# First norm and input tiles in another order, squares summed in pairs, context's row later, eight banks in the first rows, input weights by GpSimd's queue

## The chip, the cores and the metric

The kernel runs on one core of a Trainium2 chip. The metric is the device time of one execution in microseconds (us), taken as the median of several runs. Profiles and traces come from one profiled execution each.

## The reference

One block of a hybrid diffusion backbone on 512 latent tokens and 256 context tokens of width 2048, all in fp32. Only its beginning matters here:

```python
mod_l = (silu(c) @ w_ada + b_ada)          # 6 x 2048: shift, scale, gate, twice
mod_c = (silu(c_ctx) @ w_ada + b_ada)
h_l = rms_norm(x, g_mix_norm) * (1 + sc_a) + sh_a
h_c = rms_norm(ctx, g_mix_norm) * (1 + csc_a) + csh_a
qa, kva, kr, cb, cc, ch = split(h_l @ w_in)   # 2048 -> 3968 columns (31 tiles of 128, key rope twice)
...                                        # attention beside a gated convolution, output projection,
...                                        # second norm and modulation, gated MLP, final norm
```

## The kernel before

Activations lie transposed: a tile is 128 features by 512 tokens, x is sixteen of them (xs, NK = 16). Products are exact to fp32 by splitting both sides into a rounded part (hi, a cast on ScalarE) and a remainder (lo, a subtraction on VectorE) and adding three matmuls, hi-hi, hi-lo and lo-hi (mm3, lines 187 to 189). Weights are loaded into two buffers (load, tile raw), split four blocks at a time into four pairs of buffers and a spare one (split, lines 166 and 167).

At the start c is spread over the partitions by matmuls with ones and put through silu (silu_rows, lines 413 and 414), the sixteen tiles are loaded, squared on ScalarE and added up one by one on VectorE (add_squares, lines 351 to 355), context's row is treated as c was, and the norm's factor is made by rms: sums across partitions by matmuls (line 316), root and reciprocal, spread by transposes (line 299), copy to rl.

Each input tile j is then prepared by prep(j): ada(16 + j) and ada(j) load a 1 MB row of w_ada each, in two halves into four buffers (tag ada), and VectorE multiplies each half by sv = silu(c) with an accumulated sum (dot_v, line 241: four products per tile); modulate(j) scales the tile by rl (line 435), applies scale and shift on ScalarE (line 438) and splits it (hilo, lines 337 and 338).

The input projection runs in three parts of 2, 4 and 10 input tiles (KCH), each over all 31 column tiles in the order ORDER:

```python
KCH = [2, 4, 10]
K0 = [0, 2, 6]
```

In each part the first G = 6 column tiles go row by row, input tile by input tile as these become ready, on six half banks (first_banks, names pf); the other 25 go column tile by column tile (names pp). Results of the first part are copied out by ScalarE (acc), later parts are added to acc by VectorE (evac). Tiles 2 to 15 are prepared between the column tiles by the table todo, and the third part also multiplies all rows of w_ada by svc = silu(c_ctx) (ctx_mods).

Within each engine the order is set by a scheduler that goes by dependencies, except where keep() fixes it; the fetches of this stage are kept in program order on SyncE's queue (fetch_to, line 145), the weights (names rf, rw) among the modulation rows (names ada). sv is also stored to memory once, for the MLP's gate (line 1009).

## Time and profile before

| | |
|---|---|
| median of 3 runs (lowest, highest) | 2137.75 us (2131.43, 2138.17) |
| profiled execution, its own time | 2139.37 us |
| its span | 2137.6 us |
| mean granted TensorE clock, share of full | 0.993 |
| busy: TensorE, VectorE, ScalarE, GpSimd | 2091.0, 1826.5, 1047.5, 117.2 us |
| moved by DMA | 513.75 MB, 240 GB/s over the span |

The busy time of an engine is the sum over the whole execution; shares differ much between stages. The first 100 us, in which the norm is made and the input projection starts, are the stage that the change touches. In the trace's names PE is TensorE (PEld its weight load), DVE is VectorE, ACT is ScalarE, POOL is GpSimd, SP is SyncE, and a name with q is that engine's queue.

### The profile page before, as it was taken

How to read it: one execution, taken by the hardware profiler on the slowest of the kernel's cores; microseconds unless marked ns; L12 is line 12 of the kernel's file. 1: busy time of each engine (PE TensorE's matmuls, PEld its weight loads, DVE VectorE, ACT ScalarE, POOL GpSimd, SP SyncE). 2: the span in 40 equal slices, each digit the busy share in tenths (PEclk: the TensorE clock that was granted, in tenths of full speed). 3: DMA queues.
4: the chain of work that ended last, by engine and by line, in shares of the span. 5: the costliest groups of instructions: out<-in, count | busy, mean ns of one | idle time of the engine just before them, and what ended most of it. 6: DMA issues, size and time to landing. Idle time of an engine off the chain costs nothing.

```text
span 2137.6 us, 35318 instructions
## 1 busy us (share of the span) xinstructions
PE 2091.0 (98%) x13268; PEld 1881.8 (88%) x13268; DVE 1826.5 (85%) x3024; ACT 1047.5 (49%) x1715; POOL 117.2 (5%) x144
## 2 busy tenths in 40 slices
PE   7999999999999999999999999999999999999997
PEld 4688788888988888999999999999999889999997
DVE  7998987778896989898999999999999658888887
ACT  5533333555552337565555555555655433333445
POOL 0000000000000100011000000000000000000000
PEclk9999999999999999999999999999999999999999
DMA  8989886334459986577788888788888989878684
GB/s 331 343 279 329 276 275 195 126 128 152 166 188 353 348 283 220 142 217 207 230 238 232 233 233 244 224 234 234 235 229 229 362 306 307 250 231 239 197 236 134
DMA packets 170177, 513.75 MB, mean 240 GB/s; under 512 B 18963, under 2 KB 23315, under 8 KB 164371
## 3 DMA queue, kind: packets, MB, share of 16 engines
q1 hardware_dynamic: 133364, 418.14, 57.7%
q0 software_dynamic: 17408, 59.25, 14.1%
q10 hardware_dynamic: 19232, 34.09, 4.2%
q8 instruction: 104, 1.70, 0.3%
q14 instruction: 69, 0.56, 0.1%
HBM read 464.22 MB, written 46.14 MB: 239 GB/s over the span
## 4 chain that ended last, share of the span: by engine, by line
PE 90%; DVE 4%; DMA 3%; ACT 2%; issue 1%; SPq 0%; DVEq 0%; ACTq 0%; POOLq 0%
PE pp L187 4%; PE pp L189 4%; PE pp L188 4%; PE d L187 1%; PE o L187 1%; PE d L188 1%; PE o L188 1%; PE d L189 1%; PE o L189 1%; PE uf L187 1%; PE uf L189 1%; PE uf L188 1%; PE of L187 1%; PE of L188 1%; PE of L189 1%; PE pf L188 1%
## 5 line engine op out<-in xcount | busy, mean ns | idle before, releaser
L1151 POOL DMA_DIRECT2D u_s<-in_w_up x80 | 68.6, 857 | 684.0 <-DMA u_s<-in_w_up 378.1
L263 DVE SCALAR_TENSOR_TENSOR ada<-ada,sv 128x1024 f32<-128x1024 f32 x68 | 82.1, 1220 | 11.4 <-DMA ada<-in_w_ada 11.2
L166 ACT CAST w_0h<-rw 128x512 fp32r<-128x512 f32 (+1 forms) x63 | 38.3, 618 | 108.3 <-PE pp L188 67.6
L241 DVE SCALAR_TENSOR_TENSOR ada<-ada,sv 128x1024 f32<-128x1024 f32 x64 | 77.6, 1220 | 2.2 <-DMA ada<-in_w_ada 2.1
L530 DVE SCALAR_TENSOR_TENSOR ada<-ada,svc 128x1024 f32<-128x1024 f32 x64 | 76.0, 1219 | 2.5 <-DMA ada<-in_w_ada 2.4
L167 DVE TENSOR_TENSOR w_0l<-rw,w_0h 128x512 fp32r<-128x512 f32 (+1 forms) x63 | 42.7, 683 | 22.8 <-ACT w_0h L166 22.6
L263 DVE SCALAR_TENSOR_TENSOR ra<-ra,sv 128x1024 f32<-128x1024 f32 x44 | 52.5, 1219 | 1.1 <-DMA ra<-in_w_ada 1.1
L1265 DVE TENSOR_TENSOR u<-u,u_s 128x1024 f32<-128x1024 f32 x40 | 48.8, 1220 | 0.7 <-DMA u_s<-in_w_up 0.5
L1266 DVE TENSOR_TENSOR u<-u,u 128x1024 f32<-128x1024 f32 x40 | 48.7, 1218 | 0.0
L793 POOL TENSOR_TENSOR gr<-gr,half 128x8 f32<-128x8 f32 x4 | 10.1, 2524 | 630.1 <-DVE gr L792 538.2
L764 ACT CAST pth<-t 128x384 fp32r<-128x384 f32 x64 | 28.6, 485 | 26.4 <-PE t L761 26.4
L1075 DVE TENSOR_TENSOR tp<-a,tp 128x256 fp32r<-128x256 f32 x90 | 37.7, 419 | 3.3 <-ACT tp L1074 3.3
L1074 ACT CAST tp<-a 128x256 fp32r<-128x256 f32 x90 | 35.7, 403 | 5.5 <-DMA yl6h<-y_d 4.2
L1038 ACT ACTIVATE g<-g 128x512 f32<-128x512 f32 x43 | 27.3, 634 | 18.3 <-DVE g L1032 18.0
L541 DVE TENSOR_TENSOR acc<-acc,pp 128x512 f32<-128x512 f32 x50 | 34.1, 683 | 2.1 <-PE pp L189 2.1
L765 DVE TENSOR_TENSOR ptl<-t,pth 128x384 fp32r<-128x384 f32 x64 | 33.2, 550 | 2.6 <-ACT pth L764 2.6
L745 DVE TENSOR_REDUCE mn<-s 128x1 f32<-128x768 f32 x32 | 30.4, 953 | 4.9 <-PE s L734 4.6
L1030 ACT ACTIVATE g<-cg,sm 128x512 f32<-128x512 f32 x40 | 32.6, 815 | 0.0
L1030 ACT ACTIVATE a<-ca,sm 128x512 f32<-128x512 f32 x40 | 32.1, 802 | 0.0
L748 ACT ACTIVATE p<-s,mn 128x768 f32<-128x768 f32 x32 | 29.3, 916 | 1.6 <-DVE mn L745 1.3
L1031 DVE SCALAR_TENSOR_TENSOR g<-cg,sm,g 128x511 f32<-128x511 f32 x40 | 29.8, 746 | 0.0
L1032 DVE SCALAR_TENSOR_TENSOR g<-cg,sm,g 128x511 f32<-128x511 f32 x40 | 29.8, 746 | 0.0
(10238 smaller groups left out, 8925.0 us busy)
## 6 DMA issues: line engine op xcount, KB each, us to landing
ada<-in_w_ada SPq DMA_DIRECT2D x196, 512.0 KB, 5.7
u<-in_w_up SPq DMA_DIRECT2D x120, 512.0 KB, 8.9
w<-t_d SPq DMA_DIRECT2D x161, 256.0 KB, 5.3
u_s<-in_w_up SPq DMA_DIRECT2D x80, 512.0 KB, 4.0
u_s<-in_w_up POOLq DMA_DIRECT2D x80, 512.0 KB, 9.6
t_d<-tp ACTq DMA_DIRECT2D x126, 256.0 KB, 5.9
v<-in_w_dnw SPq DMA_DIRECT2D x72, 384.0 KB, 5.1
ra<-in_w_ada SPq DMA_DIRECT2D x22, 1024.0 KB, 4.8
```

What stands on the lines that cost most here:

```text
L166: A.copy(out=hi[:, :n], in_=raw[:, a:a + n])
L167: V.tensor_tensor(out=lo[:, :n], in0=raw[:, a:a + n], in1=hi[:, :n].bitcast(F32), op=ALU.subtract)
L187: PE.matmul(ps, w[0], x[0], start=first, stop=False, skip_group_check=on_top)
L188: PE.matmul(ps, w[0], x[1], start=False, stop=False, skip_group_check=on_top)
L189: PE.matmul(ps, w[1], x[0], start=False, stop=last, skip_group_check=on_top)
L241: V.scalar_tensor_tensor(out=r, in0=r, scalar=1.0, in1=vec[:, i * 1024:(i + 1) * 1024], op0=ALU.mult, op1=ALU.mult, accum_out=col[:, i:i + 1])
L263: keep(V.scalar_tensor_tensor(out=r, in0=r, scalar=1.0, in1=svs[i], op0=ALU.mult, op1=ALU.mult, accum_out=lc[:, t % 4:t % 4 + 1] if i else ...
L530: keep(V.scalar_tensor_tensor(out=raw[q], in0=raw[q], scalar=1.0, in1=svc[:, q * 1024:(q + 1) * 1024], op0=ALU.mult, op1=ALU.mult, accum_o ...
L1030: A.activation(u, src, AF.Identity, bias=s("fb", m), scale=s("fw", 86 + m))
L1151: G_.dma_start(r[-1], src[more], accum_op=ALU.add)
L1265: V.tensor_tensor(out=a11, in0=a11, in1=s1, op=ALU.add)
L1266: V.tensor_tensor(out=a12, in0=a12, in1=a11, op=ALU.add)
```

## The change

- The constants and c are fetched by ScalarE's queue; SyncE's begins with the input tiles. The two halves of modulation row 16 go between tiles 9 and 12, those of row 0 behind tile 15, then the small constants and the first weights in two halves.
- Squares: tiles 5, 9 and 13 are squared by VectorE, the others by ScalarE; two squares are added, and the pair's sums across partitions are taken at once by four matmuls that accumulate. The table for the root is loaded early.
- The first tile has a function of its own, first_tile, in a fixed order: it is scaled by the spread factor straight from the bank, and the activation is done twice, once into the rounded part. A small copy on GpSimd waits for row 0's result, ahead of that queue's loads.
- In the first part eight column tiles go row by row (GCH = [8, 6, 6]), so 23 are left; the array w_in is laid out accordingly. The casts of this part's other weights are held behind the second tile's split.
- Context's row is fetched at the second part's start, spread over the partitions by the fetch itself, and put through silu in one activation after that part's first rows.
- All further weights of the input projection are fetched by GpSimd's queue.
- The store of sv keeps its place in program order, at the end of the output projection.

```diff
+GCH = [8, 6, 6]
...
-    def first_banks(nm):
-        turn[:] = 5, None
+    def first_banks(nm, n):
+        turn[:] = (5 if n == 6 else 0), None
         r = [sml(f"{nm}{g}") for g in range(4)]
-        b = big(f"{nm}4")
-        return r + [b[:, :512], b[:, 512:]]
+        for g in range(4, n, 2):
+            b = big(f"{nm}{g}")
+            r += [b[:, :512], b[:, 512:]]
+        return r
...
-        fetch_to(raw[:, :n], src)
+        if E is not None:
+            keep(E.dma_start(raw[:, :n], src))
+        elif halves:
...
+        def first_tile():
+
+            for t in (16, 0):
+                keep(total(cols[t], t, mod[:, t:t + 1]))
+            keep(G_.tensor_copy(out=tiny(1, "late"), in_=mod[:, 0:1]))
+            sc = tiny(1, "sc0")
+            scale_of(sc, s("g_mix", 0), mod[:, 16:17])
+            x = xs[0]
+            keep(V.tensor_tensor(out=x, in0=x, in1=rs[:, 512:], op=ALU.mult))
+            hi, lo = (t2([P, T], F32R, f"h0{z}") for z in "hl")
+            w = [split_hi(raw0, 0, 512, "wf_0")]
+            keep(A.activation(hi, x, AF.Identity, bias=mod[:, 0:1], scale=sc))
+            keep(A.activation(x, x, AF.Identity, bias=mod[:, 0:1], scale=sc))
+            for a in (4, 8, 12):
+                w.append(split_hi(raw0, a * P, 512, f"wf_{a}"))
+            keep(A.copy(out=rl, in_=rs[:, 512:]))
+            split_lo(*w[0])
+            keep(V.tensor_tensor(out=lo, in0=x, in1=hi.bitcast(F32), op=ALU.subtract))
+            for z in w[1:]:
+                split_lo(*z)
+            hl[0] = hi, lo
+            return [part(z[:2], q) for z in w for q in range(4)]
...
-        for j in range(NK):
...
-            ssq = add_squares(ssq, xs[j], T, f"xs{j}")
-        silu_rows(c_ctx, svc, "cc")
...
+        for j in range(0, NK, 2):
+            q = square(j)
+            if j == 2:
+                for g in range(4):
+                    keep(A.activation(sv[:, g * 512:(g + 1) * 512], cps[g], AF.Silu))
+            r = square(j + 1)
+            if j == 12:
+                keep(A.activation(tiny(1, "root"), eps, AF.Sqrt))
+            keep(V.tensor_tensor(out=q, in0=q, in1=r, op=ALU.add))
+            for g in range(4):
+                PE.matmul(rs[:, g:g + 1], q[:, g * P:(g + 1) * P], ones[:, 0:1], start=j == 0 and g == 0, stop=j == NK - 2 and g == 3)
+            if j in (10, 12):
+                dot_half(16, j // 2 - 5, cols[16])
+        rr = tiny(4, "rr")
+        keep(A.activation(rr, rs[:, :4], AF.Sqrt, bias=eps, scale=1.0 / D))
+        keep(V.reciprocal(rr, rr))
+        spread(rs[:, 512:], rr)
+        for i in range(2):
+            dot_half(0, i, cols[0])
...
+            if ci == 1:
+                fetch_to(svc, c_ctx[0].partition_broadcast(P))
...
-                    raw = load(w_in[:, off:off + 2 * G * P], 2 * G * P, f"rf{ci}{q}")
...
+                        raw = load(w_in[:, off:off + 2 * Gc * P], 2 * Gc * P, f"rf{ci}{q}", G_)
...
+                keep(A.activation(svc, svc, AF.Silu))
...
-                    raw = load(w_in[:, off:off + k * P], k * P, f"rw{ci}_{m}")
...
+                    raw = load(w_in[:, off:off + k * P], k * P, f"rw{ci}_{m}", G_)
...
+                    with ExitStack() as behind_made:
+                        if ci == 0:
+                            for ins in second:
+                                behind_made.enter_context(tc.issue_after(ins))
...
-    SP.dma_start(sv_d, sv)
+    keep(SP.dma_start(sv_d, sv))
```

On VectorE, from the last squares to the first tile, the program before has this (xs0t the running sum, ada the halves of rows 16 and 0, rr the norm's factor):

```order
L355 TENSOR_TENSOR xs0t<-xs0t,xs_184 128x512
L455 TENSOR_SCALAR sm<-sm 128x4
L355 TENSOR_TENSOR xs0t<-xs0t,xs_189 128x512
L241 SCALAR_TENSOR_TENSOR ada_227,dvl_231<-ada_227,sv 128x1024
L241 SCALAR_TENSOR_TENSOR ada_229,dvl_231<-ada_229,sv 128x1024
L235 SCALAR_TENSOR_TENSOR mod<-dvl_231,sm 128x1
L241 SCALAR_TENSOR_TENSOR ada_235,dvl_239<-ada_235,sv 128x1024
L282 SCALAR_TENSOR_TENSOR sc_244<-mod,sm 128x1
L241 SCALAR_TENSOR_TENSOR ada_237,dvl_239<-ada_237,sv 128x1024
L235 SCALAR_TENSOR_TENSOR mod<-dvl_239,sm 128x1
L291 RECIPROCAL rr<-rr 128x4
L167 TENSOR_TENSOR wf_0l<-rf_251,wf_0h 128x512
```

The same place now, up to the scaling of the first tile by the factor in the bank rs:

```order
L526 SCALAR_TENSOR_TENSOR ada_134,dvl_159<-ada_134,sv 128x1024
L519 TENSOR_TENSOR xs_222<-xr_144 128x512
L537 TENSOR_TENSOR xs_220<-xs_220,xs_222 128x512
L526 SCALAR_TENSOR_TENSOR ada_140,dvl_159<-ada_140,sv 128x1024
L537 TENSOR_TENSOR xs_232<-xs_232,xs_234 128x512
L544 RECIPROCAL rr<-rr 128x4
L526 SCALAR_TENSOR_TENSOR ada_150,dvl_160<-ada_150,sv 128x1024
L526 SCALAR_TENSOR_TENSOR ada_152,dvl_160<-ada_152,sv 128x1024
L244 SCALAR_TENSOR_TENSOR mod<-dvl_159,sm 128x1
L244 SCALAR_TENSOR_TENSOR mod<-dvl_160,sm 128x1
L293 SCALAR_TENSOR_TENSOR sc_262<-mod,sm 128x1
L449 TENSOR_TENSOR xr_114<-xr_114,rs 128x512
```

Two of the four products now stand among the squares, and the reciprocal ahead of the other two.

On ScalarE at the second tile (xr the tile under activation, h1h its rounded part, w_..h weight casts, acc a copy out of a bank), before:

```order
L438 ACTIVATE xr_117<-xr_117,mod,sc_300 128x512
L166 CAST w_13_0h<-rw_13_337 128x512
L166 CAST w_15_0h<-rw_13_337 128x512
L166 CAST w_17_0h<-rw_13_337 128x512
L337 CAST h1h<-xr_117 128x512
L539 COPY acc_325<-pf_222 128x512
```

And now:

```order
L479 ACTIVATE xr_116<-xr_116,mod,sc_328 128x512
L481 CAST h1h<-xr_116 128x512
L175 CAST w_15_0h<-rw_15_375 128x512
L175 CAST w_17_0h<-rw_15_375 128x512
L175 CAST w_23_0h<-rw_23_511 128x512
L631 COPY acc_359<-pf_252 128x512
```

The tile's cast has moved ahead of three weight casts.

On SyncE's queue around the start of the second part, before (rf weights, ada modulation halves, kc constants):

```order
L145 DMA ada_854<-in_w_ada 128x1024
L145 DMA ada_921<-in_w_ada 128x1024
L145 DMA rf_717<-in_w_in 128x1536
L145 DMA ada_923<-in_w_ada 128x1024
L145 DMA ada_929<-in_w_ada 128x1024
L145 DMA ada_931<-in_w_ada 128x1024
L145 DMA rf_767<-in_w_in 128x1536
L145 DMA kc<-in_consts 128x1152
```

The weights of the first and second part now stand on GpSimd's queue, behind a copy that waits for row 0's result:

```order
L445 COPY late<-mod 128x1
L159 DMA rw_15_375<-in_w_in 128x2048
L159 DMA rw_23_511<-in_w_in 128x2048
L159 DMA rw_6_623<-in_w_in 128x1792
L159 DMA rf_734<-in_w_in 128x1536
L159 DMA rf_784<-in_w_in 128x1536
L159 DMA rw_13_842<-in_w_in 128x2048
```

SyncE's queue keeps the modulation halves, and the two rf loads that stood among them have moved to the other queue.

## Rows read from the trace of the kernel before

**Rows 1.** The page: the chain that ended last, shares of the span by engine.
```profile
PE 90%; DVE 4%; DMA 3%; ACT 2%; issue 1%; SPq 0%; DVEq 0%; ACTq 0%; POOLq 0%
```

**Rows 2.** Windows: width, busy us (instructions) by engine, granted clock, DMA share, GB/s.
```profile
0.00:10.00 10.00, 5.57 (x6) 1.94 (x7) 2.01 (x5) 6.59 (x10) 0.20 (x4) 1.00 0.75 242
10.00:20.00 10.00, 6.28 (x8) 2.11 (x7) 8.83 (x15) 8.17 (x16) 0.00 (x0) 1.00 1.04 402
20.00:30.00 10.00, 6.11 (x17) 3.50 (x16) 9.02 (x19) 6.25 (x11) 0.00 (x0) 1.00 1.02 416
30.00:40.00 10.00, 9.23 (x27) 6.17 (x26) 8.54 (x18) 2.89 (x5) 0.00 (x0) 1.00 0.82 326
40.00:50.00 10.00, 10.00 (x43) 8.15 (x44) 8.58 (x18) 4.95 (x9) 0.00 (x0) 1.00 0.81 257
50.00:60.00 10.00, 6.86 (x22) 4.67 (x21) 8.56 (x15) 5.34 (x10) 0.00 (x0) 0.76 1.01 403
60.00:80.00 20.00, 17.69 (x70) 13.42 (x69) 17.32 (x38) 11.20 (x21) 0.00 (x0) 0.95 0.81 272
80.00:100.00 20.00, 19.04 (x82) 15.12 (x82) 18.56 (x38) 12.64 (x22) 0.00 (x0) 1.00 1.01 399
100.00:120.00 20.00, 20.00 (x88) 16.21 (x87) 20.00 (x38) 6.56 (x12) 0.00 (x0) 1.00 0.83 281
160.00:200.00 40.00, 40.00 (x174) 32.43 (x173) 33.15 (x65) 17.18 (x30) 0.00 (x0) 1.00 0.90 311
```

**Rows 3.** Timeline of the first 40 us: start, duration, engine, line, operation, idle before.
```profile
1.58 9.56 SPq L145 DMA_DIRECT2D xr<-in_xt  x16
...
8.68 10.25 DVE L355 TENSOR_TENSOR xs0t<-xs0t,xs 128x512 f32<-128x512 f32 x13 [1.73 <-ACT xs L354]
...
19.64 1.22 DVE L241 SCALAR_TENSOR_TENSOR ada<-ada,sv 128x1024 f32<-128x1024 f32 x1
...
22.76 1.86 PE L316 MATMUL rs<-io,xs0t 128*128 128x1 f32 x8
...
23.48 1.28 ACT L289 ACT_TABLE_LOAD   x1
...
25.31 1.11 PE L299 MATMUL rs<-io,rr 128*128 128x128 f32 x4 [0.68 <-DVE rr L291]
...
28.11 0.81 ACT L438 ACTIVATE xr<-xr,mod,sc 128x512 f32<-128x512 f32 x1 [1.04 <-DVE xr L435]
...
29.63 2.07 PE L187 MATMUL pf<-h0h,wf_0h 128*128 128x512 f32 x4 [3.21 <-ACT h0h L337]
...
35.67 1.65 ACT L166 CAST w_0h<-rw 128x512 fp32r<-128x512 f32 x3
...
37.89 0.73 PE L187 MATMUL pf<-h1h,wf_4h 128*128 128x512 f32 x2 [0.33 <-ACT h1h L337]
```

**Rows 4.** The chain in order of time, at 44 us: start, duration, piece.
```profile
43.96 8.89 DMA rw<-in_w_in
```

**Rows 5.** DMA issues of the whole execution: count, KB each, median us to landing.
```profile
u_s<-in_w_up SPq DMA_DIRECT2D x80, 512.0 KB, 4.0
u_s<-in_w_up POOLq DMA_DIRECT2D x80, 512.0 KB, 9.6
t_d<-tp ACTq DMA_DIRECT2D x126, 256.0 KB, 5.9
...
rw<-in_w_in SPq DMA_DIRECT2D x25, 640.0 KB, 6.2
...
x_d<-x POOLq DMA_DIRECT2D x14, 256.0 KB, 6.3
```

**Rows 6.** Tiles h2 and h6, their pp matmuls: durations, first and last start.
```profile
L188 PE MATMUL pp<-h2l,w_0h x25: 390/393/404, 104.5 to 172.4; 128*128 128x512 f32 x25
...
L188 PE MATMUL pp<-h6l,w_0h x25: 390/392/404, 216.1 to 398.0; 128*128 128x512 f32 x25
```

**Rows 7.** The page: a costly group, busy us and mean ns, idle before.
```profile
L167 DVE TENSOR_TENSOR w_0l<-rw,w_0h 128x512 fp32r<-128x512 f32 (+1 forms) x63 | 42.7, 683 | 22.8 <-ACT w_0h L166 22.6
```

More of the change, by code (lines that the diff above doesn't have):

```diff
@@ L147, in fetch_to, with load @@
             keep(ins)
-    def load(src, n, name):
+    def load(src, n, name, E=None, halves=False):
         nth["raw"] += 1
@@ new lines, in block_kernel, with square @@
+        for j in range(10):
+            x_load_in(j)
+        ada_half(16, 0)
+        for j in (10, 11):
+            x_load_in(j)
+        ada_half(16, 1)
+        for j in range(12, NK):
+            x_load_in(j)
+        ada_half(0, 0)
+        ada_half(0, 1)
+        fetch_to(sm, small)
+        raw0 = load(w_in[:, :2 * GCH[0] * P], 2 * GCH[0] * P, "rf00", halves=True)
+        rs = big("rs")
+        def square(j):
+            q = tmp([P, T], F32, f"xs{j}")
+            if j in (5, 9, 13):
+                keep(V.tensor_tensor(out=q, in0=xs[j], in1=xs[j], op=ALU.mult))
+            else:
+                keep(A.activation(q, xs[j], AF.Square))
+            return q
@@ new lines, in dot_half @@
+        def dot_half(t, i, col):
+            r = ada_0[t, i]
+            keep(V.scalar_tensor_tensor(out=r, in0=r, scalar=1.0, in1=svs[i], op0=ALU.mult, op1=ALU.mult, accum_out=col[:, i:i + 1]))
+        cols = {t: tiny(2, f"dvl{t}") for t in (16, 0)}
+        for j in range(0, NK, 2):
[11 more added lines that the diff above has]
+                dot_half(16, j // 2 - 5, cols[16])
```

83 lines of the change are left out of this document (53 added, 30 removed).

## The prediction

> **What bounds the kernel now.** I read the chain that ended last first: TensorE has 90% of it [rows 1], so a microsecond comes off only where TensorE waits or runs slowly. The windows show where that is. From 100 us on, TensorE does 88 matmuls in 20.00 us, 0.227 us each, with no gap; between 30 and 100 us it does 27, 43, 22, 70 and 82, together 244, where that rate gives 308 [rows 2]. That is 64 matmuls or 14.5 us lost, and all of the change's arithmetic lies in or before this stretch. VectorE is the second engine to watch: it is busy 20.00 of 20 us right behind it (100 to 120), has 8.4 us idle between 30 and 100, and 6.9 us between 160 and 200 [rows 2].
>
> The timeline says what the first matmul waits for. The sixteen input tiles are fetched first; VectorE adds their squares one by one, thirteen adds in 10.25 us, and only when that ends, near 19.7 us, does it turn to the modulation products (1.22 each). Sums across partitions start at 22.76, are held by a table load (23.48, 1.28), and are spread at 25.31 in 1.11. The first matmul starts at 29.63 and the first of the second tile at 37.89, behind three weight casts that stand at 35.67 ahead of that tile's own cast [rows 3]. Later the chain goes through one weight load: issued by SyncE at 43.96, it took 8.89 us [rows 4]. Around it the window 50 to 60 has 22 matmuls and a mean granted clock of 0.76, a mixture of the 2.4 and 1.2 GHz levels, and 60 to 80 has 0.95 [rows 2].
>
> **The change part by part.**
>
> *Start of the first tile.* By 10 us the transfers moved 242 GB/s over 10 us, 2.42 MB, and 402 to 416 GB/s after that [rows 2]. SyncE's first input load stood at 1.58 behind the constants and c [rows 3]; these go to ScalarE's queue, and I take 0.8 us for it. The constants (0.13 MB), sixteen tiles (4.19 MB) and the two halves of modulation row 16 now sent among them (1.05 MB) make 5.37 MB: 9.2 + (5.37 - 2.42)/0.402 = 16.5 us until the last tile is there. Then one square, as long as a cast (0.6), one pair's add (0.69) end at 17.8. Four sum matmuls instead of eight and no table load take the stretch from 22.76 to the reciprocal (about 2.5 before the spread at 25.31) down to 1.4: half of 1.86 goes, and the rest of the table load behind it. The reciprocal ends near 19.2. Row 0's halves land at 16.5 + 1.05/0.402 = 19.1. VectorE's two products on them (2.44), which the order puts behind the reciprocal, end at 21.7; the spread (1.11) runs beside them. Three tiny operations and the scaling of the tile, 1.3 together, reach 23.0; the activation now writes the rounded tile itself (0.81). First matmul: about 24.0 instead of 29.63, and the first weights (behind row 0, the small constants and with their own half 7.2 MB in all) are due at 9.2 + (7.2 - 2.42)/0.402 = 21.1, so not late. The pairs take 11 operations instead of 15 from VectorE; that lies under the loads and I count it as nothing: without that cover it is 4 x 0.69 = 2.8.
>
> *The second tile.* What is late next is VectorE. Behind the scaling it has five remainders (0.68 each, one waits for the second activation, which ends at 24.7), to 27.6; then four products (4.9), three tiny ones (0.5) and the scaling (0.7), to 33.7. The activation and the tile's cast, which the order now puts ahead of the weight casts (1.65 for three), take 0.81 and 0.6. That gives 35.3 against 37.89: 2.6 us. By the order 24 instead of 18 matmuls stand ahead of it, since eight banks are used; six more done is 6 x 0.227 = 1.4. **Term one: 2.6 + 1.4 = 4.0**, between 1.4 (the second tile no earlier) and 5.6 + 1.4 = 7.0 (the whole of the start kept).
>
> *Weight loads by GpSimd's queue.* 42 loads leave SyncE's queue, where each waits behind the modulation loads in front of it and they behind it. The second weight load can go when the first buffer's last remainder is done, 27.6 us; with the issue and even the 8.89 us of [rows 4] it lands near 37, and TensorE needs it some 40 matmuls after 35.3. So the stop around 52 us goes: 3.1 us idle in the window 50 to 60, and the low clock, 0.24 x 10 + 0.05 x 20 = 3.4 us [rows 2]. **Term two: 6.5**, between 0 (the load is as late there) and 9.8 (the other idle time of 60 to 100, 2.3 + 1.0 us, goes too). The order keeps ScalarE's copies between casts, to which that remaining idle time belongs, so I keep it at 6.5.
>
> How long does a plain load by GpSimd's queue take? The trace has none. A plain store by it took 6.3 us, one of the same size by ScalarE's queue 5.9, a ratio of 1.07; the accumulating load of u_s took 9.6 against 4.0 by SyncE, a ratio of 2.4 [rows 5]. Applied to the 6.2 us of a 640 KB weight load, that is 6.6 or 14.9 us. These loads do not accumulate, so I take 6.6. In the long third part a block of weights is used up in (398.0 - 216.1)/24 = 7.58 us [rows 6]; with two buffers the landing and about 2.3 us of casts and remainder (1.65 + 0.68 [rows 3, 7]) must fit into 2 x 7.58, so a landing of up to 12.8 us costs nothing.
>
> VectorE runs without a gap while many of these loads are issued [rows 2], and the trace shows no plain load by this queue beside it. The Trainium skill, SBUF — State Buffer, Summary: rules for kernel authors, advises against this very move: descriptors of GpSimd's queue can't be written while VectorE holds the port the two share, so loads that are to hide beside VectorE belong on another queue. By it the time would be that of the slower rival below; by the stores' row it is that of this sum. The same page, Who interferes with whom, has copies and tensor_scalar take that port for descriptors and not tensor_tensor, and VectorE here runs products, subtractions and adds, which is why I give it a small chance only.
>
> *What it costs.* (a) Between 32 and 35.3 us TensorE has nothing to do: 24 matmuls, the first dozen at half rate as the 27 of the window 30 to 40 suggest, end near 32. Whether the clock falls again I cannot see; after the stop at 52 it did, for 3.4 us. **Term three: -1.7**, between 0 and -3.4. (b) Context's row comes as 1.05 MB spread over the partitions instead of 8 KB, 2.6 us of transfers near 65 us, and its silu, with a table load (1.28), sits on ScalarE as one block of about 3 us ahead of the cast of tile 7. VectorE then idles some 2 to 3 us. Tile 7 is first used in the third part, near 170 us, so this comes out of VectorE's 6.9 us there and costs nothing; without that cover 3 us. (c) The store of sv, 1.05 MB, moves from 16 us to ahead of the up projection's first weights: 0 to 2.6 us, and since those loads stand in the queue anyway I take **term four: -0.3**. The four matmuls of context's row leave TensorE before 23 us, where it waits anyway: nothing.
>
> Sum: 4.0 + 6.5 - 1.7 - 0.3 = **8.5 us less**. The profiled execution took 2139.37 us (span 2137.6), so 2130.9; the median of the three runs is 1.6 below it, so **2129.2**, written 2129.
>
> **The rivals.**
> - *VectorE takes it back.* Its work up to the end of the second part is the same, and at the second tile it is only about 1.5 us ahead of before (27.6 with the first tile's remainder done, against 28 without). Only if its 8.4 us of gaps close can it follow TensorE. These depend on the same transfers: up to 100 us 33.9 MB were moved [rows 2], which at 402 GB/s takes 84 us, so there is room, but not much. If the gaps stay, TensorE stands at VectorE's adds in the second part and keeps 1.5 to 4 us: **2135**. For it speaks the full 100-to-120 row, against it the 6.9 us idle behind.
> - *TensorE runs through.* If clock and remaining idle time also come right, 4.0 + 9.8 = 13.8: **2124**. It needs the transfers near 402 GB/s throughout.
> - *Slower: weights late from GpSimd's queue.* With 14.9 us for a landing a block takes (14.9 + 2.3)/2 = 8.6 instead of 7.58 us; 25 blocks lose 25.5 us, less 8.5 won: **2155**. It costs something from 12.8 us on and has eaten the gain at 13.5. The ratio of 2.4 speaks for it, the 1.07 of the plain store against. The Trainium skill's advice weighed above would be its mechanism.
> - *It doesn't do what it says*: the first tile then waits for bytes instead of adds. If the transfers run at the 326 GB/s of 30 to 40 us [rows 2] instead of 402, the 4.0 MB after 9.2 us take 12.3 instead of 10.0 us, the start gains 2.3 less, and the sum is 6.2: **2131.5**.
>
> **How the numbers follow.** A difference under 0.3%, 6.4 us, can't be told from no change here; the three runs alone span 6.7. Forecast 0.50 (its own range 2125 to 2133), VectorE 0.20, run-through 0.13, bytes 0.09, slower 0.08. Of the forecast some 0.07 lies above 2131.3. Faster is 0.43 + 0.13 + 0.04 (half of bytes) = 0.60, slower 0.08, the same 0.32. The range 2122 to 2137 leaves out the slower case and the ends of the others, some 0.15.
>
> **What would show it.** Right: the first matmul at 23 to 25 us, the second tile's at 34 to 36.5; weight loads on GpSimd's queue landing in under 9 us; no window before 100 us under 35 matmuls in 10 us except the first two; the second part's first pp matmul of this kind (104.5) near 96 and the third's (216.1) near 207 [rows 6]; a constant shift from there on. Wrong: landings over 12.8 us; TensorE waiting for an add of acc on VectorE between 95 and 165 us; a new stretch at 1.2 GHz longer than before's; ScalarE's silu of context's row in the chain.

## The result and the profile after

The changed kernel took **2142.3 us** in the median of 9 runs (2140.1 to 2146.1), the kernel before 2135.9 in 9 runs beside it (2131.4 to 2138.9): a ratio of **1.0034, 95% interval 1.0023 to 1.0046**, slower by some 7 us. The prediction was 2129 with a range to 2137. The two profiled executions differ by less, 2141.71 against 2139.37, because the one of before was a long one: of 109 further runs of that kernel, made beside the experiments with medians of 2133 to 2135, 10 took longer. This matters below.

The page of the changed kernel, the chain that ended last: TensorE has two points less than in [rows 1], and DMA two more.

```profile
PE 88%; DMA 5%; DVE 4%; issue 2%; ACT 1%; SPq 0%; DVEq 0%; POOL 0%; POOLq 0%; ACTq 0%
```

Windows of the changed kernel, columns as in [rows 2] (width; busy us and instructions of PE, PEld, DVE, ACT, POOL; granted clock; DMA share; GB/s):

```profile
10.00:20.00 10.00, 9.87 (x41) 8.33 (x39) 6.34 (x10) 7.51 (x13) 0.00 (x0) 1.00 1.04 405
20.00:30.00 10.00, 6.67 (x31) 6.19 (x30) 6.44 (x15) 2.21 (x5) 0.88 (x2) 1.00 0.67 251
30.00:40.00 10.00, 8.56 (x24) 6.49 (x24) 8.15 (x16) 3.74 (x7) 0.55 (x1) 1.00 0.96 331
40.00:50.00 10.00, 8.27 (x35) 6.45 (x36) 8.52 (x17) 7.92 (x16) 0.00 (x0) 1.00 0.82 280
50.00:60.00 10.00, 10.00 (x45) 8.10 (x43) 8.97 (x18) 3.43 (x6) 0.53 (x1) 1.00 0.88 296
60.00:80.00 20.00, 15.28 (x56) 11.13 (x55) 15.28 (x35) 11.86 (x23) 1.05 (x2) 0.91 0.95 355
80.00:100.00 20.00, 19.33 (x84) 15.38 (x83) 18.30 (x37) 13.69 (x22) 0.93 (x2) 1.00 0.86 311
```

The stop around 52 us is gone (45 matmuls in 50 to 60, 22 before), as foretold. But 60 to 80 has 56 instead of 70. TensorE stood there for ScalarE's copies out of the banks, longest at 62.72, and the window has a mean clock of 0.91:

```profile
62.72 0.51 PE L196 MATMUL pp<-h0h,w_0h 128*128 128x512 f32 x1 [2.34 <-ACT acc L631]
```

And the two windows ahead of the first tile show what was not foretold: TensorE is busy 9.87 of 10 us where little but sums is to be done, and VectorE only 6.34 and 6.44 where it had 8.83 and 9.02.

The timeline of the changed kernel's start says what that is, beside [rows 3] (start, duration, engine, line, operation, idle before and its releaser):

```profile
4.36 7.16 PE L422 MATMUL c<-c,io 1*128 1x512 f32 x8 [4.36 <-DMA io<-in_consts]
...
5.67 0.69 DVE L537 TENSOR_TENSOR xs<-xs,xs 128x512 f32<-128x512 f32 x1 [4.75 <-ACT xs L521]
...
8.15 0.60 ACT L533 ACTIVATE sv<-c 128x512 f32<-128x512 f32 x1 [1.11 <-PE c L422]
...
11.45 14.11 PE L539 MATMUL rs<-io,xs 128*128 128x1 f32 x64
...
12.71 0.69 DVE L537 TENSOR_TENSOR xs<-xs,xs 128x512 f32<-128x512 f32 x1 [6.35 <-ACT xs L521]
...
21.89 0.69 DVE L537 TENSOR_TENSOR xs<-xs,xs 128x512 f32<-128x512 f32 x1
...
25.60 0.26 ACT L543 ACTIVATE rr<-rs,eps 128x4 f32<-128x4 f32 x1 [4.49 <-PE rs L539]
25.89 0.18 DVE L544 RECIPROCAL rr<-rr 128x4 f32<-128x4 f32 x1 [3.32 <-ACT rr L543]
...
30.17 2.07 PE L196 MATMUL pf<-h0h,wf_0h 128*128 128x512 f32 x4 [2.93 <-ACT h0h L452]
...
40.73 1.19 PE L196 MATMUL pf<-h1h,wf_8h 128*128 128x512 f32 x4 [2.00 <-ACT h1h L481]
```

TensorE spreads c over the partitions until 11.5 us, and then runs 64 records of sum matmuls without a gap for 14.1 us. Three of ScalarE's four silus of c wait 1.1 us each for that spreading and hold the squares behind them, so VectorE adds its first pair at 5.67 and its second only at 12.71. Its last add is done near 22.6, and the root still waits until 25.60, for TensorE. The first matmul comes at 30.17 (29.63 before), the second tile at 40.73 (37.89 before).

Further on, the answers to [rows 5] and [rows 6], and TensorE's wait in the third part:

```profile
rw<-in_w_in POOLq DMA_DIRECT2D x25, 640.0 KB, 5.9
```
```profile
L197 PE MATMUL pp<-h2l,w_0h x25: 390/398/404, 105.0 to 173.0; 128*128 128x512 f32 x25
...
L197 PE MATMUL pp<-h6l,w_0h x25: 389/393/404, 216.9 to 400.5; 128*128 128x512 f32 x25
```
```profile
226.94 0.50 PE L198 MATMUL pp<-h6h,w_0l 128*128 128x512 f32 x1 [2.46 <-DVE w_0l L176]
```

and the same wait in the kernel before:

```profile
224.71 0.50 PE L189 MATMUL pp<-h6h,w_0l 128*128 128x512 f32 x1 [1.06 <-DVE w_0l L167]
```

The loads by GpSimd's queue land as fast as SyncE's did (5.9 against 6.2 us). The second and third part start where they did (105.0 and 216.9 against 104.5 and 216.1), and the third ends 2.5 us later.

VectorE's part in this is seen in its busy time and in its waits for modulation loads up to 175 us, of the kernel before (windows with VectorE alone: width, busy us, clock, DMA share, GB/s; waits: total, times, longest):

```profile
0.00:30.00 30.00, 19.86 (x37) 1.00 0.94 353
30.00:100.00 70.00, 61.56 (x124) 0.95 0.90 333
100.00:175.00 75.00, 75.00 (x143) 1.00 0.83 291
```
```profile
DVE ada L241 <- DMA ada<-in_w_ada: 2.1, 4, 0.9
```

and of the changed kernel:

```profile
0.00:30.00 30.00, 13.57 (x27) 1.00 0.84 310
30.00:100.00 70.00, 59.22 (x118) 0.98 0.90 320
100.00:175.00 75.00, 73.72 (x141) 1.00 0.83 293
```
```profile
DVE ada L250 <- DMA ada<-in_w_ada: 8.2, 6, 2.3
```

VectorE did 9.9 us less by 175 us (146.5 against 156.4), with about 2.8 us less to do in the start (the prediction's four adds), and waited 8.2 us for modulation loads instead of 2.1.

### The profile page after: what moved, and what is told of

It reads as the page before. It is cut to its first block, busy times and chain, and to the rows that moved or that the text cites. A ratio compares the mean times of both kernels' runs of the same rounds, so it can differ in the third digit from the quotient of the medians.

```text
span 2139.9 us, 35406 instructions
## 1 busy us (share of the span) xinstructions
PE 2092.3 (98%) x13316; PEld 1888.3 (88%) x13316; DVE 1818.9 (85%) x3020; ACT 1047.8 (49%) x1712; POOL 138.8 (6%) x187
## 4 chain that ended last, share of the span: by engine, by line
PE 88%; DMA 5%; DVE 4%; issue 2%; ACT 1%; SPq 0%; DVEq 0%; POOL 0%; POOLq 0%; ACTq 0%
PE pp L196 4%; PE pp L198 4%; PE pp L197 4%; DMA ada<-in_w_ada 1%; PE d L196 1%; PE d L197 1%; PE d L198 1%; PE o L196 1%; PE o L197 1%; PE o L198 1%; PE uf L196 1%; PE uf L197 1%; PE uf L198 1%; PE of L196 1%; PE of L197 1%
## 5 line engine op out<-in xcount | busy, mean ns | idle before, releaser
L274 DVE SCALAR_TENSOR_TENSOR ada<-ada,sv 128x1024 f32<-128x1024 f32 x68 | 82.7, 1220 | 9.1 <-DMA ada<-in_w_ada 9.0
L250 DVE SCALAR_TENSOR_TENSOR ada<-ada,sv 128x1024 f32<-128x1024 f32 x60 | 72.4, 1215 | 8.2 <-DMA ada<-in_w_ada 8.2
L870 ACT CAST pth<-t 128x384 fp32r<-128x384 f32 x64 | 28.6, 485 | 26.4 <-PE t L867 26.4
L159 POOL DMA_DIRECT2D rw<-in_w_in x35 | 18.7, 534 | 274.5 <-DVE w_8l L176 95.5
L1144 ACT ACTIVATE g<-g 128x512 f32<-128x512 f32 x43 | 27.3, 634 | 18.0 <-DVE g L1138 17.7
```

Source lines behind the costliest of these rows:

```text
L250: ins = V.scalar_tensor_tensor(out=r, in0=r, scalar=1.0, in1=vec[:, i * 1024:(i + 1) * 1024], op0=ALU.mult, op1=ALU.mult, accum_out=col[:, ...
L274: keep(V.scalar_tensor_tensor(out=r, in0=r, scalar=1.0, in1=svs[i], op0=ALU.mult, op1=ALU.mult, accum_out=lc[:, t % 4:t % 4 + 1] if i else ...
```

## The experiments

**Theories.** (1) TensorE's queue of small sum matmuls, and c's silus behind it, hold the start. (2) The store of sv, now kept ahead of the up projection's first weights, costs what is lost there (first uf matmul at 819.48, 815.83 before). (3) Weights by GpSimd's queue crowd the modulation loads. (4) The third part loses its 2.5 us at the wait at 226.94. (5), formed after e7_row16_behind: VectorE's row of work bounds everything up to 180 us, and what makes it late is paid further on.

All runs in one table. The times in us are of one profiled execution each, the ratios of the medians of 5 to 12 executions; pp stands for the part's first pp matmul as in [rows 6], the wait is VectorE's for modulation loads up to 175 us. e4, e10, e12, e17 and e19 are edits of the kernel before, the others of the changed kernel.

| kernel | first matmul | second tile | 2nd part's pp | 3rd part's pp | wait | ratio to before, 95% |
|---|---|---|---|---|---|---|
| before | 29.6 | 37.9 | 104.5 | 216.1 | 2.1 | 1 |
| changed | 30.2 | 40.7 | 105.0 | 216.9 | 8.2 | 1.0034 (1.0023 to 1.0046) |
| e1_sums_v | 33.4 | 43.9 | 109.7 | 221.3 | 9.5 | 1.0047 (1.0035 to 1.0059) |
| e6_silu_late | 29.9 | 40.5 | 102.3 | 216.4 | 6.4 | 1.0026 (1.0010 to 1.0041) |
| e5_sums_v_silu_late | 28.5 | 39.0 | 102.9 | 214.4 | 7.1 | 1.0013 (1.0002 to 1.0023) |
| e7_row16_behind | 27.1 | 37.7 | 99.3 | 214.4 | 8.5 | 1.0037 (1.0022 to 1.0052) |
| e14_quads | 26.9 | 39.2 | 100.4 | 212.7 | 4.7 | 1.0017 (1.0007 to 1.0028) |
| e2_store_early | 30.3 | 40.8 | 104.7 | 216.2 | 7.9 | 1.0035 (1.0023 to 1.0047) |
| e4_before_store_late | 31.4 | 39.1 | 101.9 | 213.5 | 4.0 | 1.0002 (0.9990 to 1.0014) |
| e3_sp_weights | 30.2 | 42.5 | 104.5 | 217.4 | 3.9 | 1.0042 (1.0028 to 1.0055) |
| e16_sums_sp | 28.6 | 41.6 | 107.4 | 219.7 | 5.3 | 1.0037 (1.0025 to 1.0050) |
| e11_row16_sp | 26.9 | 40.2 | 101.2 | 213.5 | 4.5 | 0.9995 (0.9983 to 1.0008) |
| e18_row16_late_pool | 27.0 | 39.5 | 100.6 | 212.9 | 1.9 | 0.9999 (0.9989 to 1.0010) |
| e10_before_pool | 31.1 | 42.6 | 113.7 | 226.9 | 7.7 | 1.0061 (1.0045 to 1.0078) |
| e19_before_late_pool | 29.7 | 38.0 | 102.0 | 213.5 | 1.8 | 0.9999 (0.9987 to 1.0010) |
| e12_before_more_v | 30.2 | 38.4 | 102.7 | 220.1 | 3.2 | 1.0057 (1.0038 to 1.0075) |
| e8_products_later | 29.0 | 39.6 | 103.6 | 215.2 | 4.8 | 1.0025 (1.0015 to 1.0035) |
| e15_both | 27.3 | 39.6 | 100.5 | 213.0 | 4.3 | 1.0013 (1.0003 to 1.0022) |
| e17_before_products | 29.7 | 37.9 | 101.8 | 213.3 | 3.7 | 1.0021 (1.0008 to 1.0034) |
| e9_six_banks | 30.0 | 40.0 | 105.2 | 221.7 | 9.7 | 1.0059 (1.0041 to 1.0077) |

Single executions scatter: the first matmul stands at 29.6 to 31.4 us in before, e4, e12, e17 and e19, whose program is the same up to there, at 30.2 to 30.3 in the changed kernel, e2 and e3, and at 28.5 to 29.0 in e5, e8 and e16. The 30.17 of the changed kernel is thus no earlier than before, and not clearly later.

### The start

**e1_sums_v** lets VectorE add the pairs up, with one set of sum matmuls at the end:

```diff
             keep(V.tensor_tensor(out=q, in0=q, in1=r, op=ALU.add))
-            for g in range(4):
-                PE.matmul(rs[:, g:g + 1], q[...], ones[:, 0:1], ...)
+            if j:
+                keep(V.tensor_tensor(out=q, in0=q, in1=ssq, op=ALU.add))
+            ssq = q
...
+        for g in range(4):
+            PE.matmul(rs[:, g:g + 1], ssq[...], ones[:, 0:1], start=g == 0, stop=g == 3)
```

> The changed kernel with one edit: VectorE adds the pairs' sums up, and four sum matmuls stand at the end instead of 32 spread over the pairs. Theory 1 (TensorE's queue of small sum matmuls sets the start): in the changed kernel the 64 records at L539 run without a gap from 11.45 to 25.56; here 8 records (about 1.9 us) are left and TensorE no longer ends the wait of the root. But the silus of c still hold the squares until 12.05, so VectorE starts its first pair at 12.7 as before, with 15 adds and 3 squares of about 0.61 and two products of 1.25: 12.7 + 13.5 = 26.2, plus 1.9 and 0.5 to the reciprocal at 28.5. First matmul near 32.5 (30.17 in the changed kernel), and a kernel time 0 to 3 us above it. Rival (the start waits for bytes, TensorE's queue was covered): first matmul unchanged at 30.2.

(The pair at 12.7 is the second; the first is added at 5.67, as shown above.)

**e6_silu_late** leaves the sums alone and moves only the silus of c:

```diff
-            if j == 2:
+            if j == 8:
                 for g in range(4):
                     keep(A.activation(sv[...], cps[g], AF.Silu))
```

> The changed kernel with the four silus of c behind eight of the squares instead of two; the pairs' sums stay on TensorE. Theory 1 (TensorE's queue: c's matmuls to 11.5, then 14.1 us of small sum matmuls without a gap): the sums still end near 25.6, the first matmul comes within 0.4 us of 30.17 and the time within 1.5 us of the changed kernel. Rival (the silus that hold the squares were the cause in e5_sums_v_silu_late, not the sums): first matmul 1.5 us or more earlier, the time 2 to 4 us less, like that run's.

**e5_sums_v_silu_late** has both edits.

> The run e1_sums_v with a second edit: the four silus of c stand behind eight of the squares instead of two. Theory 1 (both TensorE's small matmuls and the silus that wait for c's matmuls hold the start): VectorE starts near 5.7, works 13.5 us or follows the last tile to about 19.5, sums to 21.4, reciprocal near 22, first matmul at 26 to 27 instead of 30.17, second tile near 37 instead of 40.73. Time 3 to 4 us below the changed kernel if nothing takes it back. Rival (the modulation loads of the first 80 us set the first part anyway): first matmul as early, but the second part's first pp matmul stays at 105 and the time within 1 us of the changed kernel's 2142.3.

Alone, neither edit makes the start more than 0.3 us earlier: 33.4 us (32.5 was expected) with the sums on VectorE, which then starts late and has more to do; 29.9 with the silus late, since TensorE's row of matmuls is as long. Both together give 28.5. The first row is TensorE's sums in that run, ready at VectorE's last add and 1.87 us long; the second its first matmul:

```profile
22.01 1.87 PE L544 MATMUL rs<-io,xs 128*128 128x1 f32 x8 [10.48 <-DVE xs L539]
...
28.48 2.08 PE L196 MATMUL pf<-h0h,wf_0h 128*128 128x512 f32 x4 [2.92 <-ACT h0h L452]
```

The gain at the start was 1.7 us, less than the 3 to 4 expected, because VectorE's adds now end only at 21.9; in time it was 0.0021 x 2136 = 4.5 us. Theory 1 holds: the sum matmuls and the silus hold the start together. Of e6's time the interval is too wide to place it.

**e7_row16_behind** takes row 16's two products out of VectorE's way:

```diff
-            if j in (10, 12):
-                dot_half(16, j // 2 - 5, cols[16])
+        for i in range(2):
+            dot_half(16, i, cols[16])
         for g in range(4):
             PE.matmul(rs[:, g:g + 1], ssq[...], ...)
```

> The run e5_sums_v_silu_late with row 16's two products (1.22 each) moved from ahead of the last two pairs to behind the last add, where VectorE was idle for 2.25 us. Theory 1b (once TensorE's sums are gone, VectorE's row of work to the last add sets the start): the last add ends near 19.6 instead of 21.9, the reciprocal near 22, the first matmul at 26.0 to 26.8 instead of 28.48, the second part's first pp matmul near 101 instead of 102.9, and the time 1.5 to 2.5 us less. Rival (the last input tile lands too late for it): first matmul under 1 us earlier. Second rival (the modulation loads set the first part): first matmul earlier, but the second part at 102.5 or later, and no gain.

The first matmul came at 27.1 and the second part 3.6 us earlier than in e5, but the third part started no earlier (214.4) and the time was higher, 1.0037. TensorE waited 0.84, 0.51 and 1.04 us for weights in the second part, and longest here in the third:

```profile
225.87 0.76 PE L198 MATMUL pp<-h6h,w_0l 128*128 128x512 f32 x1 [3.83 <-DVE w_0l L176]
```

An earlier start by itself is worth nothing if VectorE cannot follow: the wait at this place grew from 2.47 us in e5 to 3.83. That VectorE is the reason is so far read from this one wait; it led to theory 5.

**e14_quads** spares VectorE three adds: two pairs are added up for each set of sum matmuls. Its base is e11_row16_sp, below.

> The run e11_row16_sp with two pairs added up on VectorE for each set of four sum matmuls on TensorE: three adds fewer on VectorE (1.83 us), three sets more on TensorE (1.87 us each, in its idle time between 11.5 and 22 us). Theory 5 (VectorE's row of work is what counts up to 180 us): the first product with context's row 1 to 2 us earlier than 173.8, time 0 to 2 us below that of e11_row16_sp (2134.5). Rival (TensorE's sets queue up again): first matmul later than 26.9 and no gain.

```diff
+        def sums(q, j):
+            for g in range(4):
+                PE.matmul(rs[:, g:g + 1], q[...], ones[:, 0:1], ...)
...
-            if j:
+            if j % 4:
                 keep(V.tensor_tensor(out=q, in0=q, in1=ssq, op=ALU.add))
+                if j < NK - 2:
+                    sums(q, j)
             ssq = q
...
+        sums(ssq, NK - 2)
```

VectorE was 0.5 us earlier at its first product with context's row (173.3 against 173.8 in e11), the first matmul where it was, and the time 1.0017, whose interval just meets that of its base: no gain, and possibly a loss that I cannot place.

### The store of sv

**e2_store_early** puts the changed kernel's store at the start of the third part; **e4_before_store_late** keeps that of the kernel before in its late place:

```diff
             if ci == 2:
+                keep(SP.dma_start(sv_d, sv))
                 bg.append(ctx_stats())
...
-    keep(SP.dma_start(sv_d, sv))
```
```diff
-    SP.dma_start(sv_d, sv)
+    keep(SP.dma_start(sv_d, sv))
```

> The changed kernel with the store of sv at the start of the third part instead of ahead of the up projection's first weights. Theory 2 (this store and the kept order around it delay the up projection's loads): the first uf matmul comes as early after the output projection as in the kernel before, 3.65 us earlier than the 819.48 of the changed kernel, less what the half-rate stretch there varies; time 2 to 4 us below the changed kernel. Rival (the loss there is the half-rate stretch that falls where it falls, not the store): the loads are issued earlier, near 808, but the end moves by under 1 us.

> The kernel before with one edit: the store of sv kept in its place in the program, ahead of the up projection's first weights, as in the changed kernel. Theory 2 (this store costs what the changed kernel loses there): the first uf matmul comes 2 to 4 us later than 815.83, and the time is 2 to 4 us above the kernel before. Rival (it is off the path, as e2_store_early suggests): within 1.5 us.

Both came out with the rival: 1.0035 beside the 1.0034 of the changed kernel, and 1.0002. Theory 2 falls. The store costs nothing that can be measured.

### The weights' queue

**e10_before_pool** puts the weights of the kernel before on GpSimd's queue; **e3_sp_weights** is the reverse on the changed kernel, back to SyncE's:

```diff
-                    raw = load(w_in[...], 2 * G * P, f"rf{ci}{q}")
+                    raw = load(w_in[...], 2 * G * P, f"rf{ci}{q}", G_)
...
-                    raw = load(w_in[...], k * P, f"rw{ci}_{m}")
+                    raw = load(w_in[...], k * P, f"rw{ci}_{m}", G_)
```

> The changed kernel with the weight loads of the input projection back on SyncE's queue. Theory 3 (weights from GpSimd's queue crowd the modulation loads, whose 8.5 us landing at 56 us and the stall of 62 to 78 us follow from it): the modulation loads land faster, the stall goes, the second part begins 2 to 5 us earlier than 105.0 and the time falls by as much. Rival (the queue is not it, and the weights were late on SyncE's queue as they were in the kernel before, where 3.1 us idle and 3.4 us of low clock followed): the second part begins 2 to 6 us later and the time rises by as much.

> The kernel before with one part of the change: the weights of the input projection by GpSimd's queue. Prediction's term two: the stop around 52 us goes and the time is up to 6.5 us less. Theory 5 (VectorE's row of work is the bound up to 180 us, and weights on a second queue make its modulation loads land later: VectorE waited 8.2 us for them up to 175 us in the changed kernel, 3.9 with the weights back on SyncE's queue): VectorE's waits for modulation loads up to 175 us rise from 2.1 to 6 us or more, the first product with context's row comes 2 to 5 us later than 173.6, and the time is 0 to 3 us more than before. Rival (no effect): both within 1 us.

Taking the queue back gave the changed kernel nothing, though VectorE's waits for modulation loads fell from 8.2 to 3.9 us: in this kernel they are not the price by themselves, and neither side of the expectation came out. The second tile came 1.8 us later (42.5), with a mean clock of 0.66 from 40 to 50 us, which may be where the shorter waits went. Given to the kernel before, the queue cost 13 us (interval 10 to 17), far more than either side expected. The transfers issued between 20 and 36 us in e10_before_pool (count, KB each, median us to landing):

```profile
ada<-in_w_ada SPq DMA_DIRECT2D x6, 512.0 KB, 9.6
rw<-in_w_in POOLq DMA_DIRECT2D x2, 1024.0 KB, 10.6
```

and in the kernel before:

```profile
ada<-in_w_ada SPq DMA_DIRECT2D x8, 512.0 KB, 6.7
rw<-in_w_in SPq DMA_DIRECT2D x1, 1024.0 KB, 9.2
```

GpSimd has nothing to do, so it issues both 1 MB loads at once, when their buffers are free, and the second of them goes 20 us before its time (23.6 instead of the 43.96 of [rows 4]):

```profile
23.64 1.09 POOL L156 DMA_DIRECT2D rw<-in_w_in  x2 [10.82 <-DVE wf_8l L170]
```

They share the DMA engines with the second tile's modulation rows, which land in 9.6 instead of 6.7 us, and six of those go out instead of eight. The second tile's first matmul falls from 37.9 to 42.6, and VectorE's wait for modulation loads rises from 2.1 to 7.7 us. SyncE's one queue was not only a place to wait in: its order was a priority. The Trainium skill, DMA: Bandwidth & Descriptors, Queues, rings and completion order, says that a DMA engine takes turns between the queues that have work, packet by packet. The landing of 9.6 us beside the 10.6 us of the two weight loads is in line with that and does not prove it.

**e16_sums_sp** is e5_sums_v_silu_late and **e11_row16_sp** is e7_row16_behind, both with the weights by SyncE's queue.

> The run e5_sums_v_silu_late with the weights back on SyncE's queue (so e11_row16_sp with row 16's products where the change has them). Theory 5 (one cause: VectorE late): waits for modulation loads fall from 7.1 to about 4 us, VectorE's milestone (first product with context's row) comes near 175 instead of 178.9, and the time is 0 to 3 us less than that of e5_sums_v_silu_late (2136.4). Rival (two causes that do not add: on SyncE's queue the weights are late as in e3_sp_weights): time within 1 us of it or above.

> The run e7_row16_behind with the weights back on SyncE's queue. Theory 5: VectorE's waits for modulation loads up to 175 us fall from 8.5 to 4 or 5 us, the first product with context's row comes 3 to 4 us earlier than 178.6, the stop of 3.83 us near 225 shrinks to 1 to 2.5, and the time is 2 to 4 us less than that of e7_row16_behind (2141.0). Rival (weights late on SyncE's queue give it back): TensorE waits for weight casts in the second part, and the time is within 1.5 us of it.

Two results that do not agree: e11 is 0.42% or 9 us faster than e7 and as fast as the kernel before, e16 is no faster than e5 but slower (1.0037, five runs of 2138.9 to 2144.5). In e16's trace the second part starts at 107.4, 6 us later than in e11, though only row 16's products stand elsewhere. 1.4 of the 6 us are lost by the second tile; after it TensorE stood 2.23 and 1.78 us for ScalarE's copies out of the banks (65.12 and 72.75) where it stood 0.49 and 0.96 in e11. What held those copies is open.

**e19_before_late_pool** and **e18_row16_late_pool** leave the first part's weights on SyncE's queue and give only the others to GpSimd's (of e10 and of e7):

```diff
-                    raw = load(w_in[...], ..., G_)
+                    raw = load(w_in[...], ..., G_ if ci else None)
```

> The kernel before with the weights of the second and third part by GpSimd's queue, those of the first part still by SyncE's. Theory 5a (the cost is in the first part, where two weight loads go at once, at 23.64 us and right behind it, ahead of the modulation rows of the second tile that VectorE waits for; in the kernel before the second of them went at 43.96): second tile near 38 as before, second part's first pp matmul at 101 to 105, time within 3 us of before, 10 us or more below e10_before_pool. Rival 5b (it costs in the second and third part too, as VectorE runs there without a gap beside this queue's loads): the third part's first pp matmul 3 us or more later behind the second's than the 111.6 us of before, and the time 5 us or more above before.

> The run e7_row16_behind with the first part's weights back on SyncE's queue and the others still by GpSimd's. Theory 5a: as e11_row16_sp, 2134.5, that is 5 to 7 us below e7_row16_behind (ratio to before 0.998 to 1.001). Rival 5b: as e7_row16_behind (ratio 1.003 to 1.005).

Both came out with theory 5a, 0.9999. VectorE's waits for modulation loads, of e19 and of e18:

```profile
DVE ada L244 <- DMA ada<-in_w_ada: 1.8, 3, 0.7
```
```profile
DVE ada L250 <- DMA ada<-in_w_ada: 1.9, 3, 0.9
```

So GpSimd's queue costs 13 us in the first part of the kernel before and 8 us in that of e7, and nothing in the second and third part, where VectorE runs without a gap beside it. The Trainium skill, SBUF — State Buffer, Summary: rules for kernel authors, which the prediction weighed, has the descriptors of such loads starve while VectorE runs in one of its 2x or 4x modes. No trace here tells VectorE's mode, and none shows the loads late: the 640 KB ones landed in 5.9 us in the changed kernel and 5.8 in e19.

### VectorE late, and six banks

**e12_before_more_v** gives the kernel before 16 useless multiplications on VectorE:

```diff
+                if ci == 1 and i < 16:
+                    keep(V.tensor_tensor(out=tmp(...), in0=rl, in1=rl, op=ALU.mult))
                 ps = bank(f"pp{ci}_{m}")
```

> The kernel before with 16 extra multiplications of 0.61 us on VectorE, one at each of the first 16 blocks of the second part, written to a scratch tile and never used: 9.8 us, as much as VectorE had done less by 175 us in the changed kernel (146.5 against 156.4 us busy). Theory 5 (VectorE being late is what the third part pays for): the first product with context's row comes 8 to 10 us later than 173.6, the stop near 224 grows from 1.06 to 2 us or more, a stretch at 1.2 GHz follows it, and the time is 2 to 5 us more than before. Rival (TensorE is the bound and VectorE's lateness is covered by its 6.9 idle us of 160 to 200): stop and time within 1 us of before.

The first product with context's row came 8.4 us later (182.0), and TensorE stood here three times as long as before:

```profile
230.98 0.50 PE L189 MATMUL pp<-h6h,w_0l 128*128 128x512 f32 x1 [3.33 <-DVE w_0l L167]
```

In place of the 2 to 5 us expected the time rose by 12 (interval 8 to 16): the 9.8 us of VectorE's time cost about all of it. No stretch at 1.2 GHz followed this wait, against the expectation. TensorE waited for weights in the second part as well, which took 117.4 us instead of 111.6 from its first pp matmul to that of the third. So far theory 5 holds: time added on VectorE in the second part is time added to the kernel, although TensorE is the one in the chain. The reverse is not shown: e14 took three adds away at the start and won nothing.

**e9_six_banks** sets the changed kernel's first rows back to six banks:

```diff
-GCH = [8, 6, 6]
+GCH = [6, 6, 6]
...
-            for a in (4, 8, 12):
+            for a in (4, 8):
                 w.append(split_hi(raw0, a * P, 512, f"wf_{a}"))
```

> The changed kernel with six banks in the first part's first rows instead of eight. Theory 5 (VectorE's row sets it): one remainder fewer stands ahead of the second tile (0.6 us), VectorE's sum of work is the same, first product with context's row within 2 us of 181.1, time within 2 us of the changed kernel. Rival (eight banks hold what TensorE gains or loses in the first part): second part's first pp matmul moved by more than 2 us from 105.0, and the time with it.

Neither side came out: it was 5 us slower than the changed kernel, with the second part's start where it was. VectorE waited 9.7 us for modulation loads, and TensorE 3.21 us at 87.9 for a weight remainder. The eight banks seem to pay, though the two intervals just meet.

### The third part's wait

**e8_products_later** (on e5), **e17_before_products** (on the kernel before) and **e15_both** (on e14) put three steps of context's products later:

```diff
-                    next(cm)
+                    if q < 7:
+                        next(cm)
...
-                    for q in range(2 if i % 4 == 0 else 1):
+                    for q in range(2 if i % 4 == 0 or i in (5, 6, 7) else 1):
```

> The run e5_sums_v_silu_late with three steps of context's modulation (a product pair each) taken from the end of the third part's first rows and put behind a few of its later blocks. In the changed kernel and in all runs on it so far TensorE stands 2.46 us near 224 for a weight remainder behind one more such pair than in the kernel before (1.06 us there), and 3.4 us at 1.2 GHz follow. Theory 4 (this costs what the third part loses: 184.2 us from h6's first pp matmul to its last, against 181.9 before): the stop and the low clock go, the third part takes 181 to 182 us, and the time is 2 to 3 us less than that of e5_sums_v_silu_late. Rival (VectorE has no room, the products only move the stop): a stop of the same size a few blocks later and the time within 1 us.

> The kernel before with three of context's product steps put later, as in e8_products_later. Theory 4: its stop of 1.06 us near 224 goes and the time is up to 1.5 us less. Rival (as in e8_products_later, later blocks or the stretch ahead of the up projection take it back): time the same within 1 us or above.

> The run e14_quads with context's last three product steps of the first rows put later, as in e8_products_later. Theory 4: the stop of 2.35 us near 223 goes, the third part stays at 181 to 182 us from h6's first to its last pp matmul, the time is 1 to 3 us less than that of e14_quads and below the kernel before by 2 to 4 us. Rival (what the third part wins is given back where the modulation loads are late, ahead of the up projection, as in e8_products_later): third part shorter, time within 1 us or above.

The wait near 224 went in all three, and in e8 the third part took 181.3 us instead of 184.2. None got faster: 1.0025 against 1.0013, 1.0021 against 1, 1.0013 against 1.0017. In e15 and e17 a wait of 2.4 us for a weight's cast stands at 310 instead. In e8 it comes back ahead of the up projection, where VectorE waited for late modulation rows and TensorE for it; the timeline of that run:

```profile
809.96 1.23 DVE L274 SCALAR_TENSOR_TENSOR ada<-ada,sv 128x1024 f32<-128x1024 f32 x1 [1.65 <-DMA ada<-in_w_ada]
...
811.66 0.69 PE L310 MATMUL rs<-io,rr 128*128 128x128 f32 x2 [3.65 <-DVE rr L302]
```

Theory 4 falls as a price. My reading is that the wait is where VectorE's lateness shows, and that moving it does not remove the lateness.

## Why the prediction was wrong

**The step that failed first** is "Four sum matmuls instead of eight ... take the stretch ... down to 1.4". I read the x8 of [rows 3] as eight matmuls. They are four, with two records each, and the change has eight sets of four: 64 records at 14.11 / 64 = 0.22 us. I also priced the last set alone, as if the other seven lay under the loads. The 1.86 us did not halve; 14.1 us took their place, behind 7.2 us of c's spreading that I had in no sum. The first matmul was forecast at 24.0 and came at 30.17. Term one, +4.0, was nothing or less: the second tile came 2.8 us later instead of 2.6 earlier. The step behind it held: from the first matmul to the second tile I had 11.3 us (24.0 to 35.3), and it took 10.6 where the kernel before took 8.3. So even the starts mended to 27 us bring the second tile to 37.7 at best (e7), against 37.9 before.

**Term two** (+6.5) was right in what it saw and wrong in what it priced. The stop at 52 us did go, the landing was 5.9 us where I took 6.6, and the rival with 14.9 is out. But the queue's effect on *other* transfers was in no term and in no rival: weights that go too early, not too late, hold back the modulation rows. That alone is 13 us on the kernel before; on the changed kernel no run shows it, since e3 won nothing. And 3.4 of the 6.5 us were the low clock of one execution. The same stretch of e4_before_store_late, a kernel that takes the same time as before, is at 2.4 GHz throughout, as it is in e12, e17 and e19:

```profile
50.00:60.00 10.00, 7.97 (x34) 5.96 (x34) 8.45 (x15) 5.34 (x10) 0.00 (x0) 1.00 1.01 389
60.00:80.00 20.00, 17.69 (x75) 13.44 (x73) 17.19 (x37) 11.81 (x22) 0.00 (x0) 1.00 0.84 291
```

Its second part starts at 101.9, that of e17 at 101.8, of e19 at 102.0 and of e12 at 102.7, where the profiled execution of before has 104.5. There was less to win than the rows on which I built.

**Term three** (-1.7) did not come at its place: TensorE was idle 2.0 us at 40.73 and the clock stayed at 1.00 up to 60 us. **Term four** (-0.3) is nothing (e4). **Part (b)**, context's row, was costed at nothing; its silu took 1.92 us behind a table load of 1.28, together 3.2 where I had about 3. It was not tried alone.

**The rival "VectorE takes it back"** came nearest, with too small a chance and price and with the wrong place: it had TensorE stand at VectorE's adds in the second part, and the changed kernel shows no such wait there; it stood for ScalarE's copies in the first part and for a weight remainder in the third. I argued that VectorE's work is the same and that it would follow if its gaps closed. They opened: its second add stood at 12.71, where thirteen adds had been running since 8.68 [rows 3], and it waited 6 us more for modulation loads. Even with both mended, e18's first matmul at 27.0 is 2.6 us earlier than that of before, its second part's pp 1.3 to 1.4 earlier than in e4 and e19, its third part's 0.6, and its time the same.

**Where the 7 us are.** Against e4, whose span of 2132.4 us stands 7.5 below that of the changed kernel: 3.1 are lost by the second part (105.0 against 101.9), 0.3 more by the third, 1.8 within it (the wait of 2.46 against 1.10 us, and a stretch of lower clock that follows it in the changed kernel), 0.8 by the output projection (630.8 against 624.8), and 1.4 up to the first uf matmul (819.5 against 812.1). The window behind that wait, in the changed kernel, columns as in [rows 2]:

```profile
226.00:232.00 6.00, 5.07 (x15) 4.02 (x16) 6.00 (x13) 0.00 (x0) 0.00 (x0) 0.72 0.91 298
```

It has 15 matmuls and a mean clock of 0.72; at 0.227 us each it would have room for 26.

Shown by runs: that sums and silus together hold the start (e1, e6, e5); that on the kernel before and on e7 the queue costs in the first part alone (e10, e19, e18); that time added on VectorE in the second part costs about one to one (e12); that the store is free (e2, e4). Only argued: that modulation rows late from sharing are how the queue costs (the rows of 20 to 36 us agree, no run separates sharing from the changed order of VectorE's work). Open: why e3 and e16 do not gain by giving the queue back while e11 does, and what context's row, the first tile's own function and the fetches by ScalarE's queue are worth, which no run has alone. No version was faster than the kernel before; e11, e18 and e19 are as fast.

## What to carry to other kernels

Before pricing a group of matmuls, divide its duration by its records and its records by the loop that issues them: "x8" can be four matmuls, and a loop moved inside another is paid once for each turn. A queue that several kinds of loads share is also their order of priority; before moving one kind to an idle engine's queue, ask which loads it will now overtake, and who waits for those, and keep the move to stretches where nobody does. And where one engine has the chain but another has no gap, price what the second loses; a stretch of low clock in one profiled execution is no term until a second execution shows it.

## What the runs showed of the hardware

A float32 matmul of a 128x128 tile by one column shows as two records of 0.22 us (14.11 us for 32 of them, 1.87 for four), so a column sum over a 128x512 tile costs TensorE 1.87 us. Spreading a 1x512 float32 row over the partitions took 7.16 / 4 = 1.79 us.

Plain loads of 640 KB by GpSimd's queue landed in 5.9 us, and beside a VectorE without a gap (100 to 175 us) they cost nothing that can be measured (e19: 0.9999, interval 0.9987 to 1.0010).
